# Attention's output kept as features by queries, its norm factors sent through DRAM as rows

## The chip, the cores and the metric

The kernel runs on one core of a Trainium2 chip. A core has five engines with their own instruction queues: TensorE (PE in the profile; its weight loads are listed as PEld), VectorE (DVE), ScalarE (ACT), GpSimd (POOL) and SyncE (SP, which here only issues DMA transfers). They run in parallel and wait for each other through semaphores; each takes its instructions strictly in its own order. The metric is the time of one execution in microseconds (us), taken on the device; lower is better.

## The reference, cut to what matters

One layer of a transformer for 256 context tokens ("prompt") and 2048 latent tokens ("sample"), model width 1024, with 4 heads of differential attention, a Fourier mixing branch, an output projection and an MLP. The part of this case is the step from the attention to the output projection:

```python
def one_block(qblk):                       # per head, 128 queries
    s = einsum('bqhmd,bkhmd->bhmqk', qblk, k) * scale
    p = softmax(s, axis=-1)
    a = p[:, :, 0] - lam * p[:, :, 1]      # two score maps, subtracted
    return einsum('bhqk,bkhe->bqhe', a, v) # 128 features a head

def merge(attn, four, subln_g, lam_init, w_out):
    a = rms_norm(attn, subln_g) * (1.0 - lam_init)   # over a head's 128 features
    return concatenate([a.reshape(b, n, 512), four], axis=-1) @ w_out
```

The norm has two parts: a factor for each query and head, the inverse root of the mean square of 128 features, and the weights subln_g x (1 - lam_init), one for each feature and the same in all heads.

## The kernel before, in words

Float32 accuracy is reached with split products: an operand is a rounded high part and a rest, and a product is three matmuls (L94, L95, L96). Stages follow each other: modulation, input projection, Fourier transforms, attention (540 to 1245 us), output projection (1245 to 1470 us), MLP.

**Attention.** For each of 4 heads, the sample's 2048 queries go in 8 groups of 256 (class Group), two blocks of 128 in each (j = 0, 1). The prompt's 256 queries of the head are one more group (class Prompt), strewn among the sample groups. For a group: PE makes scores (L1080), DVE takes row maxima, ACT exponentials with sums (L1104); POOL subtracts the second map from the first (combine: L1111, L1112, L1119, L1120); PE transposes the result (L1135, tiles pts), ACT and DVE split it into ahs and als (L1142, L1147); and PE multiplies it with V into the PSUM tile po (L94 to L96, and L1161 and L1168 for key blocks that go in one piece). The result po is features by queries: 128 features of the head on the partitions, 256 queries along the row.

Then comes what is changed here: o1, ACT copies po to oT (L1172); o2, PE transposes it back to queries by features (L1176, two transposes); o3, DVE copies that to o (L1180); o4, ACT squares it and sums along the row (L1186); o5, DVE adds the epsilon term and POOL takes the power -1/2 (L1189, L91; tile osss); o6, POOL scales o per query (L1195), and SyncE stores it to the DRAM scratch att, one tensor of 128 queries by 512 features for each token tile (L1196). The prompt's products are made with the queries stationary (L1246), so its po is queries by features at once, and it has no o1 and o2.

**What sets the order.** Every step is added to a list with a time in units of T (one of four steps of a group) and u = T / 5, and the list is sorted by it (L1350); so each engine's order is written out by numbers. The sorted order is fixed; an engine waits when its next instruction isn't ready. The tiles of a pool with a number of buffers wait until the earlier tile in that buffer is no longer used.

**The last head.** While a head runs, PE fills its time with scores of the group after next. In the last head no scores are left at the end, so that the last two groups are shorter, and POOL, ACT and DVE pass work straight to PE. The last group's o2 to o6 are put off into the output projection (list LASTO); its DMAs are issued by POOL.

**Output projection.** 18 token tiles. mix_load (L1560, L1562) loads a tile's attention part (am, from att) and its Fourier part (mT, from four, which is kept as features by tokens). mix transposes the four head blocks on PE (L1572) and ACT scales them by subln_g x (1 - lam_init), kept per partition in cols[:, 96:97] (L1573); DVE splits the result in mh and ml. out_mm multiplies with the split W_out (woh, wol, made by w_split, L1544 and L1545). The first tile is done ahead inside the attention's list (mix0_load, mix0_tr L1280, mix0_copy).

## Time and profile before

| | us |
|---|---|
| median of 3 runs (lowest to highest) | 2862.07 (2862.01 to 2862.51) |
| span of the profiled execution | 2861.4 |
| attention, 540 to 1245 us | 705 |
| output projection, 1245 to 1470 us | 225 |
| PE busy in the span | 2831.7 |

The page gives busy time and share of the span of each engine, and groups of instructions by line: engine, operation, tiles written and read with their shape, how many, total busy time and the mean of one in ns, and the idle time of the engine just before them with what ended it. The timeline view has one row for a run of like instructions: start, time from the first's start to the last's end, engine, line, and in brackets the idle time before it. A matmul's own row shows how long it is under way; matmuls overlap, so what one costs the stream is the step from its start to the next one's start. The granted TensorE clock of the profiled execution was 0.999.

### The profile page before, as it was taken

How to read it: one execution, taken by the hardware profiler on the slowest of the kernel's cores; microseconds unless marked ns; L12 is line 12 of the kernel's file. 1: busy time of each engine (PE TensorE's matmuls, PEld its weight loads, DVE VectorE, ACT ScalarE, POOL GpSimd, SP SyncE). 2: the span in 40 equal slices, each digit the busy share in tenths (PEclk: the TensorE clock that was granted, in tenths of full speed). 3: DMA queues.
4: the chain of work that ended last, by engine and by line, in shares of the span. 5: the costliest groups of instructions: out<-in, count | busy, mean ns of one | idle time of the engine just before them, and what ended most of it. 6: DMA issues, size and time to landing. Idle time of an engine off the chain costs nothing.

```text
span 2861.4 us, 43224 instructions
## 1 busy us (share of the span) xinstructions
PE 2831.7 (99%) x15109; PEld 2455.9 (86%) x15109; DVE 2018.0 (71%) x3393; ACT 1548.2 (54%) x3505; POOL 1073.3 (38%) x890
## 2 busy tenths in 40 slices
PE   8999999999999999999999999999999999999999
PEld 5888888688888888888889999999998888888887
DVE  7767886898988989864477777778775354345554
ACT  4333323798989989853356565556555332333221
POOL 1211223798999989942223333333332000000000
PEclk9999999999999999999999999999999999999999
DMA  7776777421211212036767676667747464445663
GB/s 284 219 207 198 230 213 237 172 106 38 73 71 53 106 38 99 23 124 201 242 221 232 223 246 228 221 219 238 234 167 255 147 202 135 138 144 185 206 206 111
DMA packets 392780, 492.94 MB, mean 172 GB/s; under 512 B 26467, under 2 KB 306384, under 8 KB 389490
## 3 DMA queue, kind: packets, MB, share of 16 engines
q1 hardware_dynamic: 387136, 479.73, 50.9%
q0 software_dynamic: 1872, 7.28, 0.8%
q10 hardware_dynamic: 3554, 3.17, 0.4%
q8 instruction: 119, 1.95, 0.3%
q14 instruction: 99, 0.81, 0.1%
...
## 4 chain that ended last, share of the span: by engine, by line
PE 54%; DVE 1%; DMA 0%; ACT 0%; issue 0%; SPq 0%; POOL 0%; DVEq 0%; POOLq 0%
PE ps L94 8%; PE ps L95 8%; PE ps L96 8%; PE pB L1749 2%; PE pB L1747 2%; PE pB L1748 2%; PE pA L1748 2%; PE pC L1748 2%; PE pA L1749 2%; PE pC L1747 2%; PE pA L1747 2%; PE pC L1749 2%; PE po L94 2%; PE po L96 2%; PE po L95 2%; PE pD L1749 1%
## 5 line engine op out<-in xcount | busy, mean ns | idle before, releaser
L1085 DVE TENSOR_REDUCE mxs<-Ss 128x1 f32<-128x512 f32 x636 | 405.4, 686 | 65.5 <-PE Ss L1080 55.1
L1420 DVE TENSOR_TENSOR sl<-sr,sh 128x768 fp32r<-128x768 f32 x168 | 161.8, 964 | 331.5 <-ACT sh L1419 331.1
L1120 POOL TENSOR_TENSOR P0s<-P0s,P1s 128x1024 f32<-128x1024 f32 (+2 forms) x128 | 378.6, 2958 | 10.7
L1419 ACT CAST sh<-sr 128x768 fp32r<-128x768 f32 x168 | 140.6, 838 | 418.3 <-PE ps L95 418.3
L1789 POOL TENSOR_TENSOR gs<-g,g 128x384 f32<-128x384 f32 x48 | 69.7, 1452 | 468.5 <-ACT g L1759 418.9
L1104 ACT ACTIVATE P1s<-Ss,mxs 128x512 f32<-128x512 f32 x318 | 215.4, 694 | 36.3 <-DVE mxs L1088 35.3
L94 PE MATMUL pj<-wh,hh 128*128 128x512 f32 x576 | 228.8, 397 | 2.0 <-DVE hh L555 2.0
L94 PE MATMUL ps<-thT,sh 128*128 128x512 f32 x585 | 227.6, 389 | 0.0
L95 PE MATMUL ps<-tlT,sh 128*128 128x512 f32 x585 | 227.6, 389 | 0.0
L96 PE MATMUL ps<-thT,sl 128*128 128x512 f32 x585 | 227.6, 389 | 0.0
L95 PE MATMUL pj<-wl,hh 128*128 128x512 f32 x576 | 227.1, 394 | 0.5 <-DVE wl L516 0.5
L96 PE MATMUL pj<-wh,hl 128*128 128x512 f32 x576 | 225.6, 392 | 0.0
L1104 ACT ACTIVATE P0s<-Ss,mxs 128x512 f32<-128x512 f32 x318 | 214.3, 691 | 5.6 <-DVE mxs L1088 5.0
L1135 PE MATMUL pts<-ident,P0s 128*128 128x128 f32 x1280 | 191.7, 273 | 4.5 <-DVE als L1147 1.8
L1080 PE MATMUL Ss<-KS0s,Qs 128*128 128x512 f32 x636 | 190.1, 419 | 0.4 <-ACT P1s L1104 0.4
L1080 PE MATMUL Ss<-KS1s,Qs 128*128 128x512 f32 x636 | 188.7, 420 | 1.5 <-ACT P0s L1104 1.4
L1758 ACT ACTIVATE g<-uz 128x384 f32<-128x384 f32 x144 | 75.7, 526 | 200.2 <-DVE uz L1781 174.1
L1135 PEld LDWEIGHTS pts<-ident,P0s 128*128 128x128 f32 x1280 | 151.3, 140 | 35.9 <-issue 4.8
L1119 POOL TENSOR_SCALAR P1s<-P1s,tots 128x1024 f32<-128x1024 f32 (+2 forms) x128 | 171.9, 1343 | 5.8
L1147 DVE TENSOR_TENSOR als<-pts,ahs 128x512 fp32r<-128x512 f32 x256 | 165.9, 681 | 6.9 <-ACT ahs L1142 6.7
L94 PE MATMUL ps<-ophT,sh 128*128 128x512 f32 x423 | 164.7, 389 | 1.1 <-DVE uz L1781 1.1
L96 PE MATMUL ps<-ophT,sl 128*128 128x512 f32 x423 | 164.6, 389 | 0.0
...
## 6 DMA issues: line engine op xcount, KB each, us to landing
...
a<-in_w SPq DMA_DIRECT2D x184, 256.0 KB, 4.2
...
b<-in_w SPq DMA_DIRECT2D x64, 256.0 KB, 5.8
b<-tsum SPq DMA_DIRECT2D x64, 256.0 KB, 4.7
```

The lines of the kernel that those rows point to most:

```text
L94: nc.tensor.matmul(ps, lh, rh, start=first, stop=False)
L95: nc.tensor.matmul(ps, lh, rl, start=False, stop=False)
L96: nc.tensor.matmul(ps, ll, rh, start=False, stop=last)
L1080: nc.tensor.matmul(S[:, :w], self.Q[:, x, m, j * P:j * P + P], self.hd.KS[m][:, b * 512:b * 512 + w], start=(x == 0), stop=(x == 1))
L1085: nc.vector.tensor_reduce(self.mx[j][:, m, b:b + 1], self.S[j, m, b], axis=AX.X, op=ALU.max)
L1104: nc.scalar.activation(dst, S, AF.Exp, bias=self.mx[j][:, m, 6:7], accum_out=self.sm[j][:, m, b:b + 1])
L1119: nc.gpsimd.tensor_scalar(p, p, tot[:, 3:4], 0.0, op0=ALU.mult, op1=ALU.add)
L1120: nc.gpsimd.tensor_add(d, d, p)
L1135: nc.tensor.transpose(pt[:, c:c + P], self.p0[j][:, (kb + t) * P:(kb + t + 1) * P], ident)
L1747: nc.tensor.matmul(ps, wh[:, c], hh[:, k, :], start=first and k == 0, stop=False, skip_group_check=True)
L1748: nc.tensor.matmul(ps, wh[:, c], hl[:, k, :], start=False, stop=False, skip_group_check=True)
L1749: nc.tensor.matmul(ps, wl[:, c], hh[:, k, :], start=False, stop=k == 3, skip_group_check=True)
```

## The change: what it does

The attention's output is no longer turned to queries by features.

- o1 copies po to oT as before, for the prompt too (its products now have V stationary, six matmuls of 256 queries for twelve of 128, so that its result is features by queries as well). A new step oq squares oT on ACT.
- o2 is two matmuls with one column of ones as the moving operand: the stationary operand is the squares, the result is a sum of squares for each query, two columns of the PSUM tile.
- o5 reads these columns on DVE, and POOL takes the power, as before. o3 and o4 are gone.
- o6 stores the factors to DRAM (tensor rs, 256 values of 4 bytes), o7 loads them back as a row of 256 to all 128 partitions (tile rb), and o8 multiplies oT with it on POOL and stores 128 features by 256 queries to att (one transfer of 128 KB for two of 64 KB). The squares and rb share a pool tag of two buffers.
- The times of these steps in the list are other ones; the sample groups' o6 to o8 now lie at 6.0, 9.0 and 13.6 u after o1.
- The output projection loads its features by tokens straight into mT: no transposes and no copy, for the first tile too. The norm weights go into the split of W_out: for its first four row blocks (the attention's), ACT's and DVE's split instructions take cols[:, 96:97] as a scale.

```diff
@@ -59,7 +59,8 @@
...
         qd = [scratch(f"qd{s}", [H, (NS, NP)[s] // 256, P, 2, 2, 256]) for s in range(2)]
-        att = [scratch(f"att{i}", [P, 512]) for i in range(NT // P)]
+        att = [scratch(f"att{i}", [512, 2 * P]) for i in range(NT // 256)]
+        rsd = [scratch(f"rs{h}", [NT // 256, 256]) for h in range(H)]
         four = scratch("four", [512, NT])
...
@@ -1171,29 +1172,35 @@
...
 
+                def oq(self):
+                    self.osq = self.op.tile([P, 256], F32, tag="rb", name=f"osq{self.nm}", bufs=2)
+                    nc.scalar.activation(self.osq, self.oT, AF.Square)
+
                 def o2(self):
                     for j in range(2):
-                        nc.tensor.transpose(self.po[:, 256 + j * P:256 + j * P + P], self.oT[:, j * P:j * P + P], ident)
-
-                def o3(self):
-                    self.o = self.op.tile([P, 256], F32, tag="o", name=f"o{self.nm}")
-                    nc.vector.tensor_copy(self.o, self.po[:, 256:512])
-
-                def o4(self):
-                    osq = self.op.tile([P, P], F32, tag="osq", name=f"osq{self.nm}", bufs=1)
+                        nc.tensor.matmul(PRO()[:, 256 + 2 * self.hd.s + j:257 + 2 * self.hd.s + j], self.osq[:, j * P:j * P + P], ones, start=True, stop=True)
+
+                def o5(self):
                     self.oss = self.op.tile([P, 4], F32, tag="oss", name=f"oss{self.nm}")
-                    for j in range(2):
-                        nc.scalar.activation(osq, self.o[:, j * P:j * P + P], AF.Square, accum_out=self.oss[:, j:j + 1])
-
-                def o5(self):
-                    nc.vector.scalar_tensor_tensor(self.oss[:, 0:2], self.oss[:, 0:2], 1.0 / P, self.s0e, op0=ALU.mult, op1=ALU.add)
+                    nc.vector.scalar_tensor_tensor(self.oss[:, 0:2], PRO()[:, 256 + 2 * self.hd.s:258 + 2 * self.hd.s], 1.0 / P, self.s0e, op0=ALU.mult, op1=ALU.add)
                     pow_mhalf(self.oss[:, 2:4], self.oss[:, 0:2], 2)
 
+                def place(self):
+                    return nc.gpsimd if self.last else nc.sync, self.hd.tok0 // 2 + self.g
+
                 def o6(self):
-                    for j in range(2):
-                        c = slice(j * P, j * P + P)
-                        nc.gpsimd.tensor_scalar(self.o[:, c], self.o[:, c], self.oss[:, 2 + j:3 + j], 0.0, op0=ALU.mult, op1=ALU.add)
-                        (nc.gpsimd if self.last else nc.sync).dma_start(att[self.hd.tok0 + self.g * 2 + j][:, self.hd.hc], self.o[:, c])
+                    q, n = self.place()
+                    q.dma_start(rsd[self.hd.h][n].rearrange("(j p) -> p j", p=P), self.oss[:, 2:4])
+
+                def o7(self):
+                    q, n = self.place()
+                    self.rb = self.op.tile([P, 256], F32, tag="rb", name=f"rb{self.nm}", bufs=2)
+                    q.dma_start(self.rb, rsd[self.hd.h][n:n + 1].partition_broadcast(P).rearrange("p o d -> p (o d)"))
+
+                def o8(self):
+                    q, n = self.place()
+                    nc.gpsimd.tensor_mul(self.oT, self.oT, self.rb)
+                    q.dma_start(att[n][self.hd.hc], self.oT)
 
...
@@ -1235,20 +1242,17 @@
...
 
-                def mul(self, j):
+                def mul(self):
 
                     (ah, al), V = self.A[0], self.hd.V
-                    n = 0
                     for t in range(2):
-                        c = slice((t * 2 + j) * P, (t * 2 + j) * P + P)
-                        for l, r in ((ah[:, c], V[:, t, 0, :]), (ah[:, c], V[:, t, 1, :]), (al[:, c], V[:, t, 0, :])):
-                            n += 1
-                            nc.tensor.matmul(PRO()[:, 256 + j * P:256 + j * P + P], l, r, start=False, stop=(n == 6), skip_group_check=True)
-
-                def o3(self):
-                    self.o = self.op.tile([P, 256], F32, tag="o", name=f"o{self.nm}")
-                    nc.vector.tensor_copy(self.o, PRO()[:, 256:512])
-
+                        c = slice(t * 256, t * 256 + 256)
+                        for n, (l, r) in enumerate(((0, ah), (1, ah), (0, al))):
+                            nc.tensor.matmul(PRO()[:, 256:512], V[:, t, l, :], r[:, c], start=False, stop=(t == 1 and n == 2), skip_group_check=True)
+
+                def o1(self):
+                    self.oT = self.op.tile([P, 256], F32, tag="oT", name=f"oT{self.nm}", bufs=2)
+                    nc.scalar.copy(self.oT, PRO()[:, 256:512])
 
...
@@ -1268,19 +1272,11 @@
...
 
-                MIX0.extend((f32(ts[0])[:, 2 * D:2 * D + 512], f32(ts[2])[:, 4 * D:5 * D].rearrange("p (k t) -> p k t", t=P)))
-                nc.sync.dma_start(MIX0[1][:, 4:8, :], four[:, 0:P].rearrange("(k p) t -> p k t", p=P))
+                MIX0.append(f32(ts[2])[:, 4 * D:5 * D].rearrange("p (k t) -> p k t", t=P))
+                nc.sync.dma_start(MIX0[0][:, 4:8, :], four[:, 0:P].rearrange("(k p) t -> p k t", p=P))
 
             def mix0_load():
-                nc.sync.dma_start(MIX0[0], att[0])
-
-            def mix0_tr(gr):
-                MIX0.append(gr.bank("pmx0", "pt"))
-                for k in range(4):
-                    nc.tensor.transpose(MIX0[2][:, k * P:k * P + P], MIX0[0][:, k * P:k * P + P], ident)
-
-            def mix0_copy():
-                nc.scalar.activation(MIX0[1][:, 0:4, :].rearrange("p k t -> p (k t)"), MIX0[2], AF.Copy, scale=cols[:, 96:97])
+                nc.sync.dma_start(MIX0[0][:, 0:4, :], att[0][:, 0:P].rearrange("(k p) t -> p k t", p=P))
 
...
@@ -1297,9 +1293,9 @@
...
                     add(G[2 + 2 * j] + 8 * u, gp.combine, j)
-                for t, fn, *args in ((0.25, gp.tr, 0), (0.9, gp.ah), (1.4, gp.al), (15.4, gp.mul, 0), (17.0, gp.mul, 1),
-                                     (20.85, gp.o3), (39.5, gp.o4), (40.2, gp.o5), (40.6, gp.o6)):
-                    add(G[5] + (t - 5 if h == H - 1 and t > 30 else t) * u, fn, *args)
+                for t, fn, *args in ((0.25, gp.tr, 0), (0.9, gp.ah), (1.4, gp.al), (17.0, gp.mul), (20.85, gp.o1), (21.3, gp.oq),
+                                     (28.6, gp.o2), (29.9, gp.o5), (33.0, gp.o6), (44.0, gp.o7), (49.0, gp.o8)):
+                    add(G[5] + t * u, fn, *args)
                 for g in range(hd.ng):
...
@@ -1333,17 +1329,14 @@
...
                     w = base + (AVS + 5) * T + 1.0 * u
-                    for t, fn in ((0, gr.o1), (0.4, gr.o2), (0.75 if gr.last else 4.25, gr.o3), (8.5, gr.o4), (9.2, gr.o5), (9.6, gr.o6)):
+                    for t, fn in ((0, gr.o1), (0.4, gr.oq), (2.3, gr.o2), (3.3, gr.o5), (6.0, gr.o6), (9.0, gr.o7), (13.6, gr.o8)):
                         if gr.last and t:
...
             add(base - 16 * T, load_wout)
-            add(base + T + 0.7 * u, mix0_load)
-            add(base + (AVS - 1) * T + 2.5 * u, mix0_tr, gr)
-            add(base + (AVS - 1) * T + 4.45 * u, mix0_copy)
-            
+            add(base + (AVS - 2) * T + 0.7 * u, mix0_load)
             with tc.manual_schedule():
...
@@ -1541,8 +1534,12 @@
...
                 for k in range(k0, k1):
-                    nc.scalar.copy(wh[k], WOUT[k][:, c])
-                    nc.vector.tensor_sub(wl[k], WOUT[k][:, c], f32(wh[k]))
+                    if k < H:
+                        nc.scalar.activation(wh[k], WOUT[k][:, c], AF.Copy, scale=cols[:, 96:97])
+                        nc.vector.scalar_tensor_tensor(wl[k], WOUT[k][:, c], cols[:, 96:97], f32(wh[k]), op0=ALU.mult, op1=ALU.subtract)
+                    else:
+                        nc.scalar.copy(wh[k], WOUT[k][:, c])
+                        nc.vector.tensor_sub(wl[k], WOUT[k][:, c], f32(wh[k]))
 
...
@@ -1556,21 +1553,13 @@
...
             def mix_load(i):
-                am = tx.tile([P, 512], F32, tag="am", name=f"am{i}")
-                nc.sync.dma_start(am, att[i])
-                mT = tx.tile([P, 8, P], F32, tag="mT", name=f"mT{i}")
+                M[i] = mT = tx.tile([P, 8, P], F32, tag="mT", name=f"mT{i}")
+                c = i % 2 * P
+                nc.sync.dma_start(mT[:, 0:4, :], att[i // 2][:, c:c + P].rearrange("(k p) t -> p k t", p=P))
                 nc.sync.dma_start(mT[:, 4:8, :], four[:, i * P:i * P + P].rearrange("(k p) t -> p k t", p=P))
-                M[i] = am, mT
 
             def mix(i):
-                if i == s0:
-                    mT = MIX0[1]
-                else:
-                    am, mT = M[i]
-                    pm = PRO().rearrange("p (k t) -> p k t", t=P)
-                    for k in range(4):
-                        nc.tensor.transpose(pm[:, k, :], am[:, k * P:k * P + P], ident)
-                    nc.scalar.activation(mT[:, 0:4, :], pm, AF.Copy, scale=cols[:, 96:97])
+                mT = MIX0[0] if i == s0 else M[i]
                 mh = tm.tile([P, KD, P], F32R, tag="mh", name=f"mh{i}")
...
```

Three places of the order are shown, all at the end of the last head. Names: oTs, osss, rbs belong to a sample group, op, oTp, ossp and rbp to the prompt; the number behind is the group (7 is the last one, 0 for the prompt), numbers after that only count tiles. P0s_7_1 is the last group's second block. Lines after the change are some lines higher or lower than before.

POOL, from the last combination on. Before:

```order
L1119 TENSOR_SCALAR P1s_7_1_1_14566<-P1s_7_1_1_14566,tots_7_1_14422 128x1536
L1120 TENSOR_TENSOR P0s_7_1_14485<-P0s_7_1_14485,P1s_7_1_1_14566 128x1536
L91 TENSOR_TENSOR osss_5_14643<-osss_5_14643,mhalf 128x2
L91 TENSOR_TENSOR ossp_0_14647<-ossp_0_14647,mhalf 128x2
L1195 TENSOR_SCALAR os_5_14612<-os_5_14612,osss_5_14643 128x128 x2
L1195 TENSOR_SCALAR op_0_14498<-op_0_14498,ossp_0_14647 128x128 x2
L91 TENSOR_TENSOR osss_6_14810<-osss_6_14810,mhalf 128x2
L1195 TENSOR_SCALAR os_6_14779<-os_6_14779,osss_6_14810 128x128 x2
```

After, from the power of group 5 on:

```order
L92 TENSOR_TENSOR osss_5_14523<-osss_5_14523,mhalf 128x2
L1112 TENSOR_SCALAR tots_7_1_14339<-tots_7_1_14339,nlam 128x1
L1113 TENSOR_SCALAR s0es_7_13966<-tots_7_1_14339 128x1
L1120 TENSOR_SCALAR P1s_7_1_0_14475<-P1s_7_1_0_14475,tots_7_1_14339 128x512
L1121 TENSOR_TENSOR P0s_7_1_14404<-P0s_7_1_14404,P1s_7_1_0_14475 128x512
L1120 TENSOR_SCALAR P1s_7_1_1_14487<-P1s_7_1_1_14487,tots_7_1_14339 128x1536
L1121 TENSOR_TENSOR P0s_7_1_14404<-P0s_7_1_14404,P1s_7_1_1_14487 128x1536
L92 TENSOR_TENSOR ossp_0_14538<-ossp_0_14538,mhalf 128x2
L1202 TENSOR_TENSOR oTs_5_14485<-oTs_5_14485,rbs_5_14575 128x256
L1202 TENSOR_TENSOR oTp_0_14417<-oTp_0_14417,rbp_0_14648 128x256
L92 TENSOR_TENSOR osss_6_14693<-osss_6_14693,mhalf 128x2
L1202 TENSOR_TENSOR oTs_6_14659<-oTs_6_14659,rbs_6_14734 128x256
```

The power of group 5 has moved ahead of the last combination; the prompt's still stands behind it, and the two products (L1202) wait for rows that come by DMA.

SyncE's DMA issues at the same place. Before:

```order
L1196 DMA att_84<-os_5_14612 128x128
L1196 DMA att_85<-os_5_14612 128x128
L1196 DMA att_72<-op_0_14498 128x128
L1196 DMA att_73<-op_0_14498 128x128
L1275 DMA wout_13419<-att_72 128x512
L1196 DMA att_86<-os_6_14779 128x128
L1196 DMA att_87<-os_6_14779 128x128
L1560 DMA am_14952<-att_81 128x512
```

After (rs is the factors' scratch, att_78 and att_79 are the stores of groups 5 and 6, the row into wout is the first tile's load):

```order
L1193 DMA rs_84<-osss_5_14523 128x2x1
L1193 DMA rs_84<-ossp_0_14538 128x2x1
L1198 DMA rbs_5_14575<-rs_84 128x256
L1203 DMA att_78<-oTs_5_14485 128x256
L1198 DMA rbp_0_14648<-rs_84 128x256
L1203 DMA att_72<-oTp_0_14417 128x256
L1279 DMA wout_13359<-att_72 128x4x128
L1193 DMA rs_84<-osss_6_14693 128x2x1
L1198 DMA rbs_6_14734<-rs_84 128x256
L1203 DMA att_79<-oTs_6_14659 128x256
L1558 DMA mT_14863<-att_76 128x4x128
```

The row load of group 5 now stands behind the prompt's store of factors, and its store of the output behind that load.

ACT, the last group's first casts. Before:

```order
L1142 CAST ahs_7_2_14718<-pts_7_2_14711 128x512
L1172 COPY oTs_6_14743<-po 128x256
L1142 COPY ahs_7_4_14752<-pts_7_4_14738 128x512
L1142 CAST ahs_7_6_14754<-pts_7_6_14747 128x512
L1142 CAST ahs_7_8_14773<-pts_7_8_14756 128x512
```

After:

```order
L1143 CAST ahs_7_2_14632<-pts_7_2_14625 128x512
L1173 COPY oTs_6_14659<-po 128x256
L1177 ACTIVATE osqs_6_14661<-oTs_6_14659 128x256
L1143 COPY ahs_7_4_14668<-pts_7_4_14654 128x512
L1143 CAST ahs_7_6_14672<-pts_7_6_14663 128x512
L1143 CAST ahs_7_8_14696<-pts_7_8_14674 128x512
```

The square stands behind the copy, ahead of the casts. The copy's place is the old one; its buffer is one of two of the tag oT, and it is that of oTs_5, which is in use until att_78 is stored.

## The prediction

> **What bounds the kernel now.** I read the page's first and fourth parts, then the windows of the two stages that the change touches, then single groups. TensorE is busy almost all the time, and in the attention it shares that with three engines that are nearly as full.
>
> ```profile
> PE 2831.7 (99%) x15109; PEld 2455.9 (86%) x15109; DVE 2018.0 (71%) x3393; ACT 1548.2 (54%) x3505; POOL 1073.3 (38%) x890
> PE 54%; DVE 1%; DMA 0%; ACT 0%; issue 0%; SPq 0%; POOL 0%; DVEq 0%; POOLq 0%
> 540.00:1245.00 705.00, 698.11 (x4514) 589.40 (x4513) 620.41 (x1216) 631.29 (x1762) 639.99 (x514) 1.00 0.18 65
> 1245.00:1470.00 225.00, 223.17 (x1089) 185.94 (x1088) 123.54 (x166) 92.53 (x213) 59.63 (x54) 1.00 0.68 218
> ```
>
> The last two rows are 540 to 1245 us (attention) and 1245 to 1470 us (out-projection): length, then busy PE, PEld, DVE, ACT, POOL, and the granted clock. In the attention PE stands still for 6.9 us of 705, POOL for 65, or 2.0 us for each of the 32 sample groups. In the out-projection every other engine has half its time or more free. So an instruction taken from PE is worth its own length, unless the queues that feed it become later, and the place to look for that is the end of the attention, where no scores are left to fill PE.
>
> **What is removed from PE.** The 68 transposes of the attention's output in the out-projection, with the same four on the first tile:
>
> ```profile
> L1572 PE MATMUL po<-ident,am 128*128 128x128 f32 x68 | 10.2, 272 | 0.0
> 1314.35 0.44 PE po L1572 x4
> 1326.60 0.44 PE po L1572 x4
> ```
>
> The chain gives a tile's four 0.44 us, on the path, every 12.25 us. Seventeen tiles: 17 x 0.44 = **-7.4 us**. The first tile's four (L1280) are counted below. The ScalarE copy behind them and half of the loads fall off engines and queues with slack; I give them nothing. The two transposes of each sample group become two one-column matmuls:
>
> ```profile
> L1176 PE MATMUL po<-ident,oTs 128*128 128x128 f32 x64 | 14.0, 300 | 0.5 <-ACT oTs L1172 0.4
> 246.56 0.40 PE L95 MATMUL pj<-wl,hh 128*128 128x512 f32 x1
> 246.79 0.98 PE L199 MATMUL pm<-sums,quad 128*128 128x32 f32 x8
> 247.61 0.48 PE L96 MATMUL pj<-wh,hl 128*128 128x512 f32 x1
> ```
>
> The first row charges two old transposes 14.0/32 = 0.44 us a group. No one-column matmul stands in the trace. The nearest is L199, 32 columns, in plain fp32 like the new ones, eight records for four matmuls. From its start to the start of the next matmul is 0.82 us, and that next one is itself 0.08 us longer than its like: 0.90/8 = 0.11 us a record. Two new matmuls are four such records, 0.45 us, +0.01 a group, **+0.4 us** for 32. Bounds: nothing at all for a column that streams for no time, -14 us in all; and the 0.28 us that a 256-column matmul's record lasts, four times, +22 us. I stay at L199 because neither its column count nor the load beside it differs much from the new form. The Trainium skill ("TensorE: Matmul & The Clock Gate", LDWEIGHTS) puts a load of 128 columns at 107 ns, which L199's 0.11 agrees with; the same page's table of issue gaps would let a short matmul go every 25 ns, an estimate of 0.1 us a group. That second reading is the rival C below.
>
> The prompt's products change from twelve matmuls of 128 columns to six of 256:
>
> ```profile
> 671.68 0.28 PE L96 MATMUL po<-ahs,Vs 128*128 128x256 f32 x1
> 671.80 0.34 PE L1246 MATMUL po<-Vp,ahp 128*128 128x128 f32 x2
> 672.42 0.62 PE L1135 MATMUL pts<-ident,P0s 128*128 128x128 f32 x4
> ```
>
> Six of the old take 672.42 - 671.80 = 0.62 us, twelve 1.24. A 256-column matmul takes 671.80 - 671.68 = 0.12, six 0.70. That is -0.54 a head, but the prompt now needs its own sums of squares, +0.45. Four heads: **-0.4 us**.
>
> **What moves on the other engines, in the steady groups.** These rows give the means:
>
> ```profile
> L1186 ACT ACTIVATE osqs<-os 128x128 f32<-128x128 f32 x64 | 21.1, 330 | 2.1 <-DVE os L1180 1.1
> L1186 ACT ACTIVATION_READ_ACCUMULATOR osqs<-os 128x1 f32 x64 | 13.4, 209 | 0.0
> L1172 ACT COPY oTs<-po 128x256 f32<-128x256 f32 x32 | 11.9, 372 | 1.4 <-PE po L96 1.4
> L1180 DVE COPY os<-po 128x256 f32<-128x256 f32 x32 | 13.3, 416 | 0.8 <-DMA att<-os 0.7
> ```
>
> Per group ScalarE loses two squares with read-out (2 x 0.54 us) and gains one of 256 columns (about 0.4, an estimate from the copy L1172 of that size); VectorE loses a 0.42 us copy; POOL keeps its power and trades two scalings for one product. None is on PE's path. What is new is a chain of two transfers between POOL's power and POOL's product: the factors to DRAM, and back as rows over all partitions.
>
> ```profile
> 1002.15 0.34 POOL L1111 TENSOR_SCALAR tots<-tots,nlam 128x1 f32<-128x1 f32 x1
> 1011.62 0.70 POOL L91 TENSOR_TENSOR osss<-osss,mhalf 128x2 f32<-128x2 f32 x1
> 1012.43 0.72 POOL L1195 TENSOR_SCALAR os<-os,osss 128x128 f32<-128x128 f32 x2
> 1018.37 0.38 ACT L1172 COPY oTs<-po 128x256 f32<-128x256 f32 x1
> att<-os SPq DMA_DIRECT2D x62, 64.0 KB, 1.6
> rp<-in_rope ACTq DMA_DIRECT2D x16, 64.0 KB, 2.8
> mT<-four SPq DMA_DIRECT2D x17, 256.0 KB, 3.4
> ```
>
> The power goes ahead of the second half's combination, which starts at 1002.15, and the product stays where the scaling is. So the factors leave at about 1002.9 and are wanted at about 1012.3. Two hops at 1.6 (a store) and 2.8 (a load) with two issues of 0.4 are 5.2 us of the 9.4 there. The stored group's buffer is wanted again at the soonest by the next group's copy at 1018.37: product to 1013.1, store to about 1014.9, 3.5 us to spare. Cost nothing; the cover is POOL's own combination of some 9 us, and rival D is its loss.
>
> **The end of the last head.** Here the cover is gone. In the built program the sixth sample group's output takes the buffer of the fifth's (the prompt holds the other), so ScalarE's copy of it waits until the fifth has been multiplied and stored. Its norm factors come back behind the prompt's on SyncE, which stands waiting for POOL's last power.
>
> ```profile
> 1232.99 0.69 POOL L91 TENSOR_TENSOR osss<-osss,mhalf 128x2 f32<-128x2 f32 x1
> 1233.66 0.68 POOL L91 TENSOR_TENSOR ossp<-ossp,mhalf 128x2 f32<-128x2 f32 x1
> 1234.74 0.80 SPq L1196 DMA_DIRECT2D att<-os  x2
> 1235.62 0.86 SPq L1196 DMA_DIRECT2D att<-op  x2
> 1237.21 0.32 SPq L1275 DMA_DIRECT2D wout<-att  x1
> 1232.95 0.37 ACT L1172 COPY oTs<-po 128x256 f32<-128x256 f32 x1 [1.39 <-PE po L96]
> 1233.38 0.44 PE L1176 MATMUL po<-ident,oTs 128*128 128x128 f32 x2
> 1237.49 1.10 PE L1161 MATMUL po<-ahs,vf4s 128*128 128x256 f32 x4 [0.56 <-DVE os L1180]
> 1240.72 0.60 PE L1280 MATMUL pmx<-ident,wout 128*128 128x128 f32 x4
> 1245.22 0.39 PE L94 MATMUL po<-woh,mh 128*128 128x512 f32 x1
> PE po L1161 <- DVE os L1180: 1.1, 2, 0.6
> ```
>
> Before, POOL's last combination ends at 1232.99. One power of 0.69 now stands ahead of it: 1233.7. The prompt's power: 1234.4. SyncE issues the prompt's store, 0.4: 1234.8, then the fifth group's row load. I take 1.8 for that hop (between the store's 1.6 and the load's 2.8, nearer the store since it too is small and the queues are quiet): 1236.6. POOL's product, 0.74 as two scalings take now: 1237.4. Its store, 1.4: the rows show a dependent issue 1.6 us after a pair of stores began and 1.2 after the second of them: 1238.8. Copy 0.4, square 0.4: 1239.6, and PE's sums at 1239.65 instead of its transposes at 1233.38, **6.3 us late**. Queued behind the copy on ScalarE are all remaining casts of the last group, so PE, whose next products follow the sums, finds nothing to run ahead. From there to the first matmul of the out-projection stood 1245.22 - 1233.38 = 11.84 us; of these go the wait of 0.56 and the first tile's transposes of 0.44. So the out-projection starts 6.3 - 1.0 = **5.3 us late**. The other 0.56 us wait for the old copy (two in all, 1.1 us) gains nothing, since POOL sets the end here. With both hops at 1.2 it is 4.5; with 2.8 and 2.4, 7.3. What is late next: the first tile's load, behind the prompt's store at about 1240, would be in by 1244; the second tile's, behind the sixth group's store, by about 1251.5, wanted at 1256. Both are covered by the same delay. W_out's split gets a longer VectorE form for half of its rows:
>
> ```profile
> L180 DVE SCALAR_TENSOR_TENSOR macc<-wm,cols,macc 128x512 f32<-128x512 f32 x112 | 78.6, 747 | 23.2 <-DMA wm<-in_w_mod 23.1
> L1545 DVE TENSOR_TENSOR wol<-wout,woh x16: 679/684/871, 1243.5 to 1257.2; 128x512 fp32r<-128x512 f32 x16
> ```
>
> At most 4 x (0.75 - 0.68) = 0.3 us a half, on an engine that was ahead of PE there; taken as nothing.
>
> The Trainium skill ("DMA: Bandwidth & Descriptors", Anatomy of one DMA) gives each transfer about 2.0 us of fixed cost, most of it the receipt from the memory; by that the two hops are 4.0 instead of 3.2, and the sum below 0.8 us higher. The store rows' 1.6 decide here. The same page has writes under 512 bytes done as read-modify-write, which speaks against writing 256 factors of 4 bytes; no row of this trace shows such a store's price.
>
> **The sum.** -7.4 + 0.4 - 0.4 + 5.3 = -2.1 us on the profiled span of 2861.4, so 2859.3. The median of the runs lies 0.7 above that span (2862.07): **2860.0 us**. A measurement of this kernel can tell about 0.2% from no change, 5.7 us, so this is within it.
>
> **The rivals.**
> A, the forecast: two thirds of the gain are given back at the end of the last head. 0.58; alone it spans 2857 to 2864, by the hops' bounds and 2 us either way for the sums.
> B, the end hides it: the copy's wait is over before PE arrives, or ScalarE's casts don't hold PE. For it: POOL and the queues are nearly idle there. Against: the arithmetic above is 6 us from it. Then -7.4 - 0.4 (the first tile) + 0.4 - 0.4 - 1.1 = -8.9: 2853.2. 0.15.
> C, the one-column matmuls cost next to nothing: 36 groups x up to 0.45 us more on top of A, halfway -8: 2852.0. Against it stands L199's 0.11 a record. 0.08.
> D, slower: the way through DRAM is late in the steady groups. It decides from the point where the two hops take over 9.4 us rather than 5; then POOL stands before its product, and once its 2.0 us of idle a group are spent, each further microsecond is one on PE in some 28 groups. At 13 us it is (13 - 9.4 - 2.0) x 28 = +45: 2905; at 11.8 it is 0.4 x 28 = +11: 2871. For it: 4-byte pieces, unseen here, and SyncE's queue in which a waiting issue holds the next group's loads. Against: 4 us of slack. 0.12.
> E, as A with every hop at the 3.4 us of the 256 KB load: (3.4 - 1.8) + (3.4 - 1.4) = +3.6: 2863.6. 0.07.
>
> **How the numbers follow.** Faster by over 0.2% (under 2856.4): B, C and a little of A, 0.25. Slower by over 0.2% (over 2867.8): D, 0.12. Within: 0.63. The range leaves out D and the cheap end of C: 2853.0 to 2866.0.
>
> **What would show it.** Right, if the out-projection's tile period falls from 12.25 to about 11.8 us; if PE has one idle time of 5 to 7 us near 1234 to 1240 before the last sums, released by ScalarE's square; and if the sums' four records take 0.45 us. Wrong at the end, if that idle is under 2 us; wrong in the steady groups, if POOL waits for a DMA before its product or the time from one group's sums to the next's grows; wrong on the sums, if a record is far from 0.11 us.

## The result, and the profile after

The changed kernel takes 2933.47 us (median of 4 runs, 2931.50 to 2937.40) where the one before takes 2862.29 beside it: 1.025 of its time, interval 1.0236 to 1.0263. It is slower, by 71.2 us; the prediction was 2860.0 and no change. The profiled execution spans 2929.7 us, 68.3 more than before. (Run again later, e5 below, the same kernel took 2970.27.)

The page's head and its fourth part after:

```profile
span 2929.7 us, 43049 instructions
PE 52%; DVE 1%; DMA 0%; issue 0%; ACT 0%; SPq 0%; POOL 0%; DVEq 0%; POOLq 0%
```

The chain of waits is no help here: PE still leads it, as before, and everything else has 1% or less, although 68 us of new time came from other engines' lateness. The windows show the place:

```profile
540.00:1245.00 705.00, 659.98 (x4223) 558.83 (x4222) 562.24 (x1120) 583.92 (x1576) 597.61 (x445) 1.00 0.22 68
1245.00:1320.00 75.00, 56.69 (x370) 50.39 (x368) 36.64 (x69) 40.84 (x97) 42.22 (x34) 0.89 0.09 19
```

In 540 to 1245 us, PE stood still for 6.9 us before and stands still for 45.0 now; the attention then runs on until about 1313. Three marks split the kernel: ScalarE's copy o1 of the first sample group, its copy of the 29th (the first one whose successors belong to the shortened end), and the first matmul of the output projection. Before:

```profile
572.09 0.37 ACT L1172 COPY oTs<-po 128x256 f32<-128x256 f32 x1
1196.83 0.38 ACT L1172 COPY oTs<-po 128x256 f32<-128x256 f32 x1
1245.22 0.39 PE L94 MATMUL po<-woh,mh 128*128 128x512 f32 x1
```

After:

```profile
571.57 0.37 ACT L1173 COPY oTs<-po 128x256 f32<-128x256 f32 x1
1244.42 0.37 ACT L1173 COPY oTs<-po 128x256 f32<-128x256 f32 x1
1313.48 0.39 PE L95 MATMUL po<-woh,mh 128*128 128x512 f32 x1
```

| stretch (us) | before | after | difference |
|---|---|---|---|
| 28 steady groups (copy to copy) | 624.7 | 672.9 | +48.1 |
| end of the last head (copy to first matmul) | 48.4 | 69.1 | +20.7 |
| output projection and all that follows | 1616.2 | 1616.2 | 0.0 |

With the 0.5 us by which the first copy is earlier this is the 68.3. Each steady group is 1.72 us longer; the prediction had +0.01.

**In the steady groups** PE waits where it did not before. One group on the timeline of PE and VectorE:

```profile
983.02 0.50 PE L1181 MATMUL po<-ones,osqs 128*128 128x1 f32 x4
983.38 0.72 PE L1081 MATMUL Ss<-KS0s,Qs 128*128 128x512 f32 x2
984.29 0.36 PE L95 MATMUL po<-ahs,Vs 128*128 128x256 f32 x1
985.67 0.28 PE L97 MATMUL po<-ahs,Vs 128*128 128x256 f32 x1
987.01 0.63 PE L1136 MATMUL pts<-ident,P0s 128*128 128x128 f32 x4 [1.06 <-DVE als L1148]
986.04 0.16 DVE L1185 SCALAR_TENSOR_TENSOR osss<-po,s0es 128x2 f32<-128x2 f32 x1 [1.22 <-PE po L97]
986.18 1.28 DVE L1148 TENSOR_TENSOR als<-pts,ahs 128x512 fp32r<-128x512 f32 x2
```

The sums (L1181) are issued at 983.02 and followed by other matmuls from 983.38. VectorE's o5 (L1185), which reads them, starts at 986.04, released not by L1181 but by L97: the last of the next group's first products with V, which write other columns of the same tile po. VectorE stands for 1.22 us, the rests als come that much later, and PE, which needs their tile back for its next transposes, stands for 1.06. In the list o5 lies at 1.0 + 3.3 = 4.3 u, and the next group's first products at 3.9 u: they come before it. The view of waits (in all, times, longest):

```profile
PE pts L1136 <- DVE als L1148: 29.5, 27, 1.8
PE po L1181 <- ACT osqs L1177: 16.4, 2, 12.7
PE po L95 <- DVE mh L1565: 5.4, 1, 5.4
DVE osss L1185 <- PE po L97: 61.2, 30, 18.7
POOL oTs L1202 <- DMA rbs<-rs: 103.2, 28, 12.4
```

The last row is a second new wait: POOL, before its product, for the factors' row. It is the sign that the prediction named for a wrong steady group. One such group on the timeline of POOL and SyncE:

```profile
989.84 0.72 POOL L92 TENSOR_TENSOR osss<-osss,mhalf 128x2 f32<-128x2 f32 x1
990.58 0.37 SPq L1193 DMA_DIRECT2D rs<-osss  x1
999.83 0.32 SPq L1198 DMA_DIRECT2D rbs<-rs  x1
1003.51 0.73 POOL L1202 TENSOR_TENSOR oTs<-oTs,rbs 128x256 f32<-128x256 f32 x1 [3.37 <-DMA rbs<-rs]
```

The store of 256 factors leaves at 990.58 and the load that waits for it at 999.83. The store's line (L1193) and the load's row in the page's part on DMA issues give all groups, as us from issue to landing:

```profile
DMA to landing us min/median/max: 8.1/8.5/10.4
```

```profile
rbs<-rs SPq DMA_DIRECT2D x31, 128.0 KB, 4.5
```

Medians of 8.5 and 4.5, 13.0 us where the prediction had 5.2 for both.

**At the end of the last head** the chain is the predicted one, with other lengths (the timelines of SyncE, POOL, ACT and PE, put in order of time):

```profile
1289.51 0.37 SPq L1193 DMA_DIRECT2D rs<-ossp  x1
1290.05 0.34 SPq L1198 DMA_DIRECT2D rbs<-rs  x1
1297.40 0.72 POOL L1202 TENSOR_TENSOR oTs<-oTs,rbs 128x256 f32<-128x256 f32 x1 [7.91 <-DMA rbs<-rs]
1298.15 0.33 SPq L1203 DMA_DIRECT2D att<-oTs  x1
1300.09 0.37 ACT L1173 COPY oTs<-po 128x256 f32<-128x256 f32 x1 [14.07 <-DMA att<-oTs]
1300.96 1.01 PE L1181 MATMUL po<-ones,osqs 128*128 128x1 f32 x4 [12.72 <-ACT osqs L1177]
1302.94 0.41 PE L96 MATMUL po<-als,Vs 128*128 128x256 f32 x1
1303.15 0.41 PE L97 MATMUL po<-ahs,Vs 128*128 128x256 f32 x1
1325.57 0.77 PE L95 MATMUL po<-woh,mh 128*128 128x512 f32 x1 [5.43 <-DVE mh L1565]
```

Group 5's row load is issued 0.54 us behind the prompt's store of factors, and its product starts 7.35 us after that issue, against 3.7 in the group above and 4.7 in the median of the sample groups. Then come product, store, copy and square as predicted, and PE's sums stand 12.72 us. When PE starts again its products follow each other at 0.21 us (1302.94 to 1303.15) where they took 0.12 before the change; the granted clock is 0.89 over the window from 1245 to 1320 us and 0.50 from 1300 to 1304. The Trainium skill ("TensorE: Matmul & The Clock Gate", Part 1) has the clock halved after an idle window of about 3.4 us and for as long after the restart; 0.21 against 0.12 agrees. Last, the second tile's load stands behind group 6's row and store on SyncE, and the output projection waits another 5.43 us after its first tile.

### The profile page after: what moved, and what is told of

It is laid out like the page before. It is cut to its first block, busy times and chain, and to the rows that moved or that the text cites. A ratio compares the mean times of both kernels' runs of the same rounds, so it can differ in the third digit from the quotient of the medians.

```text
span 2929.7 us, 43049 instructions
## 1 busy us (share of the span) xinstructions
PE 2837.8 (97%) x15093; PEld 2464.7 (84%) x15093; DVE 1982.6 (68%) x3357; ACT 1525.2 (52%) x3383; POOL 1067.5 (36%) x855
## 4 chain that ended last, share of the span: by engine, by line
PE 52%; DVE 1%; DMA 0%; issue 0%; ACT 0%; SPq 0%; POOL 0%; DVEq 0%; POOLq 0%
PE ps L95 8%; PE ps L96 8%; PE ps L97 8%; PE pB L1738 2%; PE pB L1736 2%; PE pB L1737 2%; PE pA L1738 2%; PE pC L1737 2%; PE pA L1736 2%; PE pC L1738 2%; PE pA L1737 2%; PE pC L1736 2%; PE po L95 2%; PE po L97 2%; PE po L96 2%; PE pD L1738 1%
## 5 line engine op out<-in xcount | busy, mean ns | idle before, releaser
L97 PE MATMUL ps<-thT,sl 128*128 128x512 f32 x585 | 227.6, 389 | 0.0
L1136 PE MATMUL pts<-ident,P0s 128*128 128x128 f32 x1280 | 192.8, 274 | 35.7 <-DVE als L1148 29.5
L97 PE MATMUL pj<-wh,hl 128*128 128x512 f32 x576 | 225.3, 391 | 0.0
L1081 PE MATMUL Ss<-KS0s,Qs 128*128 128x512 f32 x636 | 197.4, 423 | 8.7 <-ACT P1s L1105 7.5
L1143 ACT CAST ahs<-pts 128x512 fp32r<-128x512 f32 x256 | 147.4, 609 | 39.3 <-PE pts L1136 39.2
```

Source lines behind the costliest of these rows:

```text
L97: nc.tensor.matmul(ps, ll, rh, start=False, stop=last)
L1081: nc.tensor.matmul(S[:, :w], self.Q[:, x, m, j * P:j * P + P], self.hd.KS[m][:, b * 512:b * 512 + w], start=(x == 0), stop=(x == 1))
L1136: nc.tensor.transpose(pt[:, c:c + P], self.p0[j][:, (kb + t) * P:(kb + t + 1) * P], ident)
```

## The experiments

Two explanations for the steady groups stood against each other. **W**: VectorE's wait on tile po, 1.06 us a group on PE, sets the 23.6 us period. **D**: the way through DRAM does; POOL's work of about 20 us and its 3 to 4 us of waiting fill the same 23.6 us, and PE's wait is what its queues show of it. The stretches of the table above, for every run:

| run | time, us | ratio (interval) | groups | end | rest |
|---|---|---|---|---|---|
| before | 2862.3 | 1 | 624.7 | 48.4 | 1616.2 |
| after | 2933.5 | 1.0250 (1.0236 to 1.0263) | 672.9 | 69.1 | 1616.2 |
| e1_sums_early | 2969.8 | 1.0373 (1.0343 to 1.0403) | 704.6 | 72.5 | 1619.9 |
| e2_old_row | 2921.9 | 1.0206 (1.0176 to 1.0236) | 669.1 | 65.4 | 1612.4 |
| e3_both | 2887.8 | 1.0087 (1.0058 to 1.0116) | 638.2 | 64.2 | 1610.4 |
| e4_own_buffer | 2962.0 | 1.0346 (1.0316 to 1.0376) | 702.0 | 67.7 | 1621.6 |
| e5_again | 2970.3 | 1.0376 (1.0355 to 1.0397) | 702.6 | 71.9 | 1618.5 |
| e6_hidden | 2886.4 | 1.0083 (1.0068 to 1.0098) | 638.8 | 52.8 | 1620.0 |
| e7_pairs | 2911.9 | 1.0172 (1.0152 to 1.0193) | 669.6 | 59.1 | 1609.0 |
| e8_filler | 2884.8 | 1.0082 (1.0065 to 1.0099) | 636.5 | 51.8 | 1621.7 |
| e9_short | 2867.1 | 1.0013 (1.0003 to 1.0023) | 635.7 | 48.4 | 1608.8 |
| e10_square | 2877.4 | 1.0047 (1.0032 to 1.0062) | 644.4 | 50.6 | 1609.3 |
| e11_later | 2874.0 | 1.0036 (1.0021 to 1.0052) | 635.7 | 49.8 | 1615.7 |
| e12_half | 2944.8 | 1.0284 (1.0263 to 1.0304) | 682.1 | 69.9 | 1617.1 |
| e13_lines | 2919.9 | one run | 669.1 | 62.7 | 1615.5 |
| e14_gaps | 3032.0 | one run | 749.7 | 78.3 | 1629.4 |
| e15_vector | 2944.6 | 1.0287 (1.0272 to 1.0302) | 706.0 | 53.2 | 1610.2 |
| e16_vector_late | 2927.2 | 1.0229 (1.0212 to 1.0246) | 688.2 | 53.7 | 1611.6 |
| e17_no_square | 2866.5 | 1.0014 (1.0004 to 1.0024) | 633.6 | 47.0 | 1612.5 |
| e18_early_sums | 2863.2 | 0.9998 (0.9988 to 1.0008) | 631.6 | 47.7 | 1612.7 |

Runs 1 to 4, 5 to 8, 9 to 12 and 13 to 18 were each made on one chip, and the kernel before ran on each (2862.3 to 2863.2); the record does not name the chip of the first result. The stretches are of one profiled execution; the first group's copy starts at 570.2 to 573.7 us in all of them. The groups of the runs in which both waits are gone and ScalarE squares at the kernel's own place (e3, e6, e8, e9, e11) differ by up to 3 us, 635.7 to 638.8, so a difference of 2 us in one column is little.

**Which of the two waits: e1, e2, e3.**

```diff
 e1: the factors' o5 ahead of the next group's products
-(3.3, gr.o5)
+(2.75, gr.o5)
 e2, in o7: the row of the group two before (the prompt's g unchanged)
+                    n -= 2 if n > 2 else 0
 e3: both
```

> One number of the order list changed: VectorE's step on the sums (o5) lies ahead of the next group's first products into the same PSUM tile instead of behind them. Theory W (VectorE's step waits for the last writer of the tile that stands before it in the list, the next group's products, and holds the casts behind it, for which TensorE then waits 1.06 us a group): the wait goes, about 30 groups x 1.1 = -33 us, 2900. Theory D (the time of a group is set by POOL, which waits for the row from DRAM): POOL's chain is as long as before, the wait only moves to another place: within 5 us of 2933.

> The row load (o7) reads the factors of two groups earlier in the head instead of the group's own (groups 0 and 1 of a head and the prompt keep their own), so that it does not wait for the store of 4-byte factors; the output's scaling is therefore another one, and nothing else changes. Theory D: POOL's idle time before its product, 3.3 us a group, goes, the group falls back to about 22.2 us: -45 us, and some -10 at the end of the last head: 2880. Theory W: TensorE's 1.06 us a group stay; -10 at the end and at most -0.4 a group: 2910 or more.

> The two edits together. If they are two waits of which either alone fills the group (each hides behind the other), only this run falls to 22.1 us a group: 2875 to 2880, the rest being the end of the last head. If one theory holds alone, this run equals that one's.

o5 then lies at 3.75 u. e1 takes W away: PE's wait for als falls from 29.5 us to 1.8, what it was before the change. The time fits neither theory's forecast. The first two groups last 22.3 to 22.4 us, but POOL's wait grows and most later ones last 23 to 30. Its waits:

```profile
PE Ss L1081 <- ACT P1s L1105: 44.6, 41, 5.7
POOL oTs L1202 <- DMA rbs<-rs: 138.2, 30, 15.7
```

e2 takes much of D away (POOL waits 62.0 us) and leaves W: the groups stay at 23.6 us, and PE's wait for als at 29.5, as in the changed kernel. What is left of D is the load itself: issued about 0.5 us behind a 4-byte store that it does not depend on, it lands after 7.8 us in the median, where it took 4.6.

```profile
DMA to landing us min/median/max: 3.4/7.8/12.5
```

e3 takes both: groups of 22.4 us, 638.2 for the 28. So neither theory alone was right: each wait by itself keeps the groups long, and both must go. With W alone 28 groups take 669 us (e2, and e7 below); with D alone they take 705 on the chip of e1. How long D alone would make them where the store is as fast as in the first result was not run.

**The end: e4, and the kernel again: e5.** The prompt's output and row get buffers of their own (pool tags that are free by then), so that the copy of group 6 does not wait for group 5's store.

```diff
-self.oT = self.op.tile([P, 256], F32, tag="oT", name=f"oT{self.nm}", bufs=2)
+self.oT = self.op.tile([P, 256], F32, tag="P1_1", name=f"oT{self.nm}", bufs=1)
 # and the prompt's osq and rb: tag ("rb", "P0_1")[self.hd.s]
```

> The prompt's output, squares and row get buffers of their own (those of its scores, idle by then), so that the sixth group's copy no longer waits for the fifth group's store. Both theories: the steady groups stay at 23.6 us; TensorE's waits of 12.7 and 3.6 us for the squares at the end of the last head go. If the first tile's load (behind the prompt's row) is not the next wait, -20 us: 2913; if it is, it starts about when the prompt's store has landed, about 1310 instead of 1325: -14 us, 2919.

> The changed kernel itself again, beside the next three: 2933 if the landing time of the 4-byte store does not differ from chip to chip; nearer to 2950 if it was the chip that made the runs with early sums and with own buffers slow (their stores landed in 8.5 to 10.6 us against 8.5).

In e4 PE's 12.72 us wait for the squares is gone, and in its place stands one for the first tiles of the output projection:

```profile
PE po L95 <- DVE mh L1565: 12.5, 2, 10.8
```

So the buffer was the cause of the 12.72, and the queue of slow transfers behind it is next. The changed kernel itself takes 2970.27 in e5, and its 28 groups 702.6 us instead of 672.9, with W's 29.5 us as they were. What differs there in the trace is D: from the store's issue to the load's it is 8.8 us in the median instead of 8.0, and the load's way to the product is 0.2 longer. e1 has the same 8.8. The kernel was not run on e1's chip, so that e1's 704.6 beside 702.6 makes it likely, not shown, that removing W alone gains nothing where the store is that slow.

**Hide the way, or shorten it: e6, e7, e8, e9.** e6 leaves the transfers as they are and moves the product, o8, to 23.6 u after o1 (13.6 in the last head's last groups), with o5 at 2.75 u, own buffers, and the last head's prompt steps earlier. e8 is e6 with o2 at 1.2 u and o5 at 1.9 u. e7 changes only how the factors lie in DRAM: pairs, so that each partition stores one piece of 8 bytes, 128 pieces for 256 of 4 bytes; POOL's product reads its operands in the matching order. e9 is e7 with o5 at 2.75 u, own buffers and the earlier prompt.

```diff
 e6
-(13.6, gr.o8)
+(13.6 if h == H - 1 and g > 3 else 23.6, gr.o8)
 e7
-rsd[self.hd.h][n].rearrange("(j p) -> p j", p=P)
+rsd[self.hd.h][n].rearrange("(p j) -> p j", p=P)
-nc.gpsimd.tensor_mul(self.oT, self.oT, self.rb)
+nc.gpsimd.tensor_mul(self.oT.rearrange("p (j q) -> p j q", j=2), self.oT.rearrange("p (j q) -> p j q", j=2), self.rb.rearrange("p (q j) -> p j q", j=2))
```

> Nothing left out. The sums' step (o5) ahead of the next products; the product (o8) 10 u later, behind the next group's first combination, so that the row has some 22 us instead of 12; the prompt's output, squares and row in buffers of their own; in the last head the prompt's factors are made earlier (o2 to o8 at 27.4, 28.4, 29.0, 34, 38 u) and groups 4 on keep 13.6 u. Two waits, each enough for 23.6 us: the steady groups fall to 22.4 us, +0.4 x 30 = +12 on before, -7.4 for the output projection, about +5 at the end: 2872. If POOL's wait for the row is not what sets the groups, they stay above 23 us: 2900 or more.

> The changed kernel with the factors stored as 128 pieces of 8 bytes instead of 256 of 4 (the row holds pairs, and the product reads it with a stride). If the landing time goes by the number of pieces: 8.5 us becomes 4 to 5, POOL's wait goes; the groups then stay at 23.6 us through VectorE's wait alone, and the end of the last head is about 8 us shorter: 2925. If it goes by something else (a fixed price, or the loads ahead in the queue): 8 us, 2933.

> As the hidden one, with the sums' matmuls at 1.2 u instead of 2.3 (where the old transposes filled a wait of TensorE for a score bank) and the sums' step at 1.9 u. If the 0.34 us that a group keeps with both waits gone is 0.17 for the sums and 0.28 for that unfilled wait, the groups fall from 22.4 to about 22.15 us: -7 us against the hidden one, 2865. If the sums then wait for the square, they stay at 22.4.

> Nothing left out: the factors in pieces of 8 bytes, the sums' step ahead of the next products (o5 at 2.75 u), the prompt's tiles in buffers of their own and its factors earlier in the last head; the product stays at 13.6 u. Both bounds of 23.6 us gone: groups of 22.4 us as with both edits that left the own row out, +0.4 x 30 = +12 on before; -7.4 for the output projection; the end between 0 and +6: 2867 to 2873. If VectorE's wait or the row still sets the groups: 23.6 us, 2905.

e7, the timeline of SyncE, the waits, and the product's group:

```profile
987.27 0.32 SPq L1193 DMA_DIRECT2D rs<-osss  x1
990.67 0.32 SPq L1198 DMA_DIRECT2D rbs<-rs  x1
```

```profile
PE pts L1136 <- DVE als L1148: 29.5, 27, 1.8
```

```profile
L1202 POOL TENSOR_TENSOR oTs<-oTs,rbs 128x256 f32<-128x256 f32 x32 | 24.8, 776 | 13.6 <-DMA rbs<-rs 13.6
```

The load now leaves 3.40 us after the store, not 9.25, and POOL's whole wait is 13.6 us. W is untouched, its 29.5 us and its 669.6 us for 28 groups too. e6 shows the other way: with the slow transfers merely hidden the groups are as short (638.8), but the end, where nothing hides them, still costs +4.4, and the output projection waits 6.7 us for its second tile. e9 has neither; its longest waits of PE, and o5 on VectorE's timeline:

```profile
PE pr L117 <- DVE rows L115: 6.2, 1, 6.2
PE Ss L1081 <- ACT P1s L1105: 4.3, 22, 0.4
```

```profile
985.44 0.15 DVE L1185 SCALAR_TENSOR_TENSOR osss<-po,s0es 128x2 f32<-128x2 f32 x1
```

The first wait is far from the attention and was there before, 6.2 us; o5 has no idle time in front of it. The end takes 48.4 us, as before the change, the rest 1608.8 instead of 1616.2, and the 28 groups 11.0 more. In sum it is 0.13% above the kernel before. The end is shorter in e7 already, where only the pieces changed: the prompt's store of factors and group 5's row load are issued 0.49 us apart as in the changed kernel, but the product follows the load's issue after 2.90 us instead of 7.35, and PE's wait for the squares is 6.38 us (12.7 in e5, on the same chip). e8's earlier sums made no difference to e6.

**What the way costs: e12, e13, e14.** Why is a store of 1 KB slow? Three stores of only the first block's 128 factors (the second block's are left out, and in e13 and e14 one factor for each partition is used): side by side as before (e12), each 64 bytes apart (e13), each 8 bytes apart (e14).

```diff
 e12
+q.dma_start(rsd[self.hd.h][n][0:P].rearrange("(p j) -> p j", j=1), self.oss[:, 2:3])
 e13 (scratch of 2048 values a group)
+q.dma_start(rsd[self.hd.h][n].rearrange("(p j) -> p j", j=16)[:, 0:1], self.oss[:, 2:3])
 e14
+q.dma_start(rsd[self.hd.h][n].rearrange("(p j) -> p j", j=2)[:, 0:1], self.oss[:, 2:3])
```

> The changed kernel, storing only the factors of a group's first 128 queries, 128 pieces of 4 bytes, and using them for both halves: the second half's own factors are left out, the output's scaling is another one. If the landing time goes by the number of pieces, it falls from 8.5 us as with 128 pieces of 8 bytes, to about 3.2 us from issue to the next issue; if a piece of 4 bytes costs more than one of 8, it lies between, 4 to 6 us. The groups stay at 23.6 us through VectorE's wait, 2912.

> The changed kernel, storing the factors of a group's first 128 queries as 128 pieces of 4 bytes, each 64 bytes from the next, and loading back eight of them; the product takes the first one for all queries, so the other factors are left out. Only the time from the store's issue to the load's issue is of interest: theory S (a piece of 4 bytes is dear by itself): 8 us as before; theory L (pieces that fall into one stretch of 64 bytes are written one after the other; sixteen did so with pieces of 4 bytes side by side, eight with pieces of 8): under 3 us.

> As the one before, each piece of 4 bytes 8 bytes from the next, eight in 64 bytes. Theory S: 8 us. Theory L: as with pieces of 8 bytes, 3 to 4 us.

The store's line in e12, then in e7, e13 and e14:

```profile
DMA to landing us min/median/max: 8.1/8.9/9.2
```

```profile
DMA to landing us min/median/max: 2.9/4.2/8.9
```

```profile
DMA to landing us min/median/max: 1.4/2.9/3.6
```

```profile
DMA to landing us min/median/max: 2.9/4.9/5.7
```

The landing can include a wait in the queue, and the forms were run on different chips (the changed kernel's own step was 8.0 us at first and 8.8 in e5). The step from the store's issue to the dependent load's is cleaner, and its median over the sample groups is:

| pieces | bytes each, spacing | pieces in 64 bytes | store issue to load issue, us |
|---|---|---|---|
| 256 (after) | 4, side by side | 16 | 8.0 |
| 128 (e12) | 4, side by side | 16 | 8.0 |
| 128 (e7) | 8, side by side | 8 | 3.3 |
| 128 (e14) | 4, every 8 | 8 | 3.2 |
| 128 (e13) | 4, every 64 | 1 | 1.45 |

Half as many pieces cost the same; twice the spacing brings 8.0 to 3.2, with pieces of 4 or of 8 bytes alike; and pieces 64 bytes apart cost 1.45, no more than the 1.2 to 1.6 us of a dependent issue behind the 64 KB stores before the change. So the price goes with how close the pieces lie, or how many of them fall into the same stretch of memory, not with their number or size. It isn't the time to hand out the pieces either: in all five forms the packets of a store's pieces are recorded within 1.2 us of its issue. That the stretch is 64 bytes long is not shown; these spacings would look the same with one of 32 or 128. The Trainium skill ("DMA: Bandwidth & Descriptors", Specifications) says that transfers below 512 bytes are done as read-modify-write. Several such writes to one stretch would have to wait for each other, which fits these rows; the serial order itself is not seen in a trace. The whole times of e13 and e14 say little, as they load a strided row: it lands 6.2 us after its issue in e13 and 11.5 in e14 (4.6 in the changed kernel), and in e14 POOL waits 199.9 us in all.

**When o5 may come: e10, e11.** Both are e9 with other times: the square at 1.3 u, sums at 2.55 u and o5 at 2.85 u (e10); o5 at 4.6 u after o1, or 5.6 in the list: behind the next group's products again, but later than the changed kernel's 4.3 (e11).

> As the short one, with the square (oq) at 1.3 u instead of 0.4, the sums' matmuls at 2.55 and the sums' step at 2.85 u. If the 0.34 us a group that stays is the square, 0.42 us on ScalarE right behind the copy, holding back the exponentials that free a score bank for TensorE: groups of 22.1 us, 2860 to 2866. If not: 22.4 us, as the short one.

> As the short one, but the sums' step is put behind the next group's first products for good, at 4.6 u instead of 2.75, where they should have ended when VectorE gets there. If VectorE's wait is only a matter of arriving about 1.1 us too soon for the tile's last writer: no wait, groups of 22.4 us, within 5 us of the short one. If the order itself costs (the step then holds casts, or POOL's power comes late): 23 us or more, 2885 or more.

e11's groups take 635.7 us, as e9's, without the wait for als. So a place behind the next products is no cost by itself: at 4.3 u VectorE arrives 1.2 us before they end, at 5.6 u, with more of its own work ahead, after they have ended. e11 loses at the end, where the factors and the tile loads queue later (PE waits 4.0 us for mh). e10's groups are 8.7 us longer; a later square helps nothing.

**The remaining 0.39 us a group: e15, e16, e17, e18.** It is e9's 11.0 us over 28 groups. These runs are e9 with other squares. In e15 VectorE makes the square instead of ScalarE (at 1.0 u), in e16 too but later (at 1.9 u, with the sums at 2.6 and o5 at 2.88). In e17 and e18 there is none: the identity is the stationary operand of the sums, so the factors are not the norm's; e18 puts the sums at 0.41 u.

```diff
 e15
-nc.scalar.activation(self.osq, self.oT, AF.Square)
+nc.vector.tensor_mul(self.osq, self.oT, self.oT)
 e17
+nc.tensor.matmul(PRO()[:, 256 + 2 * self.hd.s + j:257 + 2 * self.hd.s + j], ident, ones, start=True, stop=True)
 e18
-(2.3, gr.o2)
+(0.41, gr.o2)
```

> As the short one, the square on VectorE instead of ScalarE, at 1.0 u (VectorE has lost a copy of 0.42 us to the change, so its load is as before; ScalarE's falls by 0.42 us). If the square on ScalarE is what holds a score bank back, 0.34 us a group: groups of 22.1 us, 2858 to 2862. If the 0.36 us a group is TensorE's own order: 22.4 us, 2867.

> As the one before, the square at 1.9 u, the sums at 2.6 and the sums' step at 2.88 u. The same question with VectorE's square behind one more row maximum: 22.1 us if the place at 1.0 u delays that maximum, else no better than the one before.

> As the short one, without ScalarE's square: the sums' matmuls take the identity as their stationary operand, at the same place; the factors are therefore meaningless. If the square in front of the exponentials is what a steady group keeps over the kernel before (0.36 us, 0.17 of it the sums themselves): groups of 22.15 us, 2860. If not: 22.4 us, 2867.

> As the one before, and the sums' matmuls at 0.41 u, where the old transposes stood, ahead of TensorE's wait for a score bank. If that wait of 0.34 us is the same in both kernels and the old transposes only filled it: groups of 22.1 us here and 22.4 us in the one before. If the square alone made it, the two are equal.

e15, the timelines of VectorE and POOL around one square, and then the square's line (shortest, median and longest, in ns):

```profile
974.47 3.21 DVE L1177 TENSOR_TENSOR osqs<-oTs 128x256 f32<-128x256 f32 x1
973.93 3.46 POOL L1121 TENSOR_TENSOR P0s<-P0s,P1s 128x1536 f32<-128x1536 f32 x1
```

```profile
L1177 DVE TENSOR_TENSOR osqs<-oTs x32: 412/2998/3248, 573.9 to 1334.2; 128x256 f32<-128x256 f32 x32
```

The square takes 0.41 us at the least and 3.0 in the median: it starts during POOL's product and ends at 977.68, 0.29 us after it. So do 28 others of the 32: whenever they start within such a product, they end 0.28 to 0.29 us behind it, so that VectorE in effect waits it out. On VectorE the square thus costs PE 54.1 us of waits. The Trainium skill ("SBUF — State Buffer", Who interferes with whom) states that a VectorE instruction with two SBUF inputs contends with a GpSimd instruction that reads SBUF; the 0.41 and the 3.21 us agree. e16's square, 0.9 u later, meets the same product nearer to its end (1.98 us in the mean instead of 2.59) and is still slower than ScalarE's 0.43.

e17 shows that the square is not most of what is left: without it the time is that of e9, as the groups and the end are 3.5 us shorter and the rest 3.7 longer (there PE waits 1.1 us for a tile's mh, for which it does not wait in e9). With the sums moved to the place of the old transposes (e18) PE's waits for score banks (the row Ss <- ACT P1s) go from 5.5 us (e17) to 0.4, the groups another 2.0 us down, and the time is that of the kernel before (0.9998). So the sums' later place, which the square's time forces, costs about 0.1 us a group (3.3 us between the medians of nine runs each). The sums themselves cost 0.17, shown below. The rest of the 0.39 stays open.

## Why the prediction was wrong, by its steps

**The 68 transposes, -7.4 us: right.** With next to nothing waiting there (e9, e7) the stretch from the first matmul of the output projection to the end is 7.2 to 7.4 us shorter. The tile period, read at VectorE's cast of mh:

```profile
1385.97 0.69 DVE L1565 CAST mh<-mT 128x1024 fp32r<-128x1024 f32 x1
...
1409.52 0.69 DVE L1565 CAST mh<-mT 128x1024 fp32r<-128x1024 f32 x1
```

Two periods in 23.55 us, 11.8 each (as in the median), as predicted, from 12.25. In the changed kernel the 5.43 us wait and the lower clock behind it take all of it back.

**The sums, +0.4 us in all: the new matmuls right, the old ones mis-sized.** The four records step PE by 983.38 - 983.02 = 0.36 us (predicted 0.45). But the two transposes they replace, charged at 0.44 by their busy time, stepped it by only 0.19 before:

```profile
951.74 0.44 PE L1176 MATMUL po<-ident,oTs 128*128 128x128 f32 x2
951.93 1.22 PE L1080 MATMUL Ss<-KS0s,Qs 128*128 128x512 f32 x4
```

Here the rows' busy time is 0.25 us longer than the step, since the next matmul already runs in it; the front matter's rule, step from start to start, was not applied to this row. The term is +0.17 a group, 5 us for 32, instead of +0.4 in all. Rival C (almost free) fell. A record of the new form steps 0.09 us, near the 0.11 read from L199.

**The steady groups, "Cost nothing; the cover is POOL's own combination": wrong, and this is the step that decided.** Two things failed in it.

First the hops: 1.6 and 2.8 us from rows of large stores and loads, measured 8.0 to 8.5 and 4.5 to 4.7. The row for the store was a bad neighbour: att's pieces are 512 bytes long, rs's 4 bytes, side by side. The prediction said itself that no row showed the price, but took a value from the nearest row and gave the other end only to rival D. The price that it set beside the rows, 2.0 us a transfer, is stated there for transfers that GpSimd issues, while these go through SyncE; it is as far off. D's own point of change, 9.4 us, was right in kind: with 12.7 us POOL waits, and with 7.2 (e7: 3.3 to the load's issue and 3.9 to its landing) hardly any more. By its formula the medians of the steps, 8.0 from issue to issue and 4.7 from the load's issue to the product, would have made (12.7 - 9.4 - 2.0) x 28 = +36 us; the 28 groups took 48 more, with W in them too.

Second, a wait that no rival named: o5 reads PSUM tile po behind the next group's products, which write it too, and VectorE comes there before they end. The old reader of that tile, o3, lay behind the same products, at 1.0 + 4.25 = 5.25 u, and met no wait for PE, since they had ended by then (its row in the prediction: 0.8 us of idle time in all, 0.7 for a DMA). The change put the reader at 4.3 u, between the products' place and their end; e1, e3 and e9 (ahead of them, 3.75 u) and e11 (5.6 u) lie on either side and are both free of it. The prediction followed o5 only to POOL's power and never placed it in VectorE's list against PE's.

**The end of the last head, +5.3 us: the mechanism right, the size not.** The copy of group 6 waits for group 5's store (e4 shows it by the buffer), and everything from power to square was in the predicted order. The term that failed is again the hop, 1.8 us predicted, 7.35 measured behind the prompt's 4-byte store and 2.90 behind the same store in 8-byte pieces (e7). The wait came out at 12.72 (and another of 3.64 ahead of it) where the sums were to come 6.3 late, with the clock at 0.50 behind it, and the tile load that the prediction called covered came 5.43 us late. +20.7 and +5.4 in place of +5.3.

**The prompts, -0.4, and W_out's split: nothing of weight against them.** A head's six products step 0.72 us and its four records of sums 0.36, where twelve products took 1.24: -0.6 for four heads. The scaled split takes ScalarE 0.72 us and VectorE 0.75 to 0.81 each; PE waits for the latter only once, 0.4 us, and only in some runs (e7, e9), not in the changed kernel.

**The rivals.** D was given 0.12, with the observation that 4-byte pieces were unseen; its mechanism is one of the two in the steady groups, and its slow store is most of the loss at the end. Even with both waits gone (e9) the forecast's -2.1 is not reached, since the groups cost 11.0 us and not 0.
